# Moving a 32-row tile's products ahead of the last product of the first row pair

## The chip, the cores and the metric

The kernel runs on one core of a Trainium2 chip. A core has five engines that each take their instructions in order: TensorE (PE: matrix products, with weight loads listed as PEld), VectorE (DVE), ScalarE (ACT), GpSimd (POOL) and SyncE (SP). SP, POOL and ACT also issue DMA transfers; a transfer is "landed" when the engines that wait for it may go on. The metric is the device time of one execution in microseconds (us).

## The reference

One inference step of a small trunk, everything in float32. There are 2048 rows of a new stream (the prompt) and 32 rows of a running one (the sample), 1024 columns each. For each set of rows:

```
hn   = rmsnorm(h) * g_mix
proj = hn @ w_in                         # 1024 -> 3072, split in six parts of 512
yA   = B * (causal conv of C*h_in) * silu(zA)
yB   = (trailing means of v, minus v, mixed per group, scaled) * silu(zB)
h    = h + concat[yA, yB] @ w_out        # 1024 -> 1024: the output stage
gate = sigmoid(rmsnorm(h) * g_ple @ w_ple_gate)
h    = h + (p @ w_ple) * gate            # the gate stage
out  = rmsnorm(h) * g_final
```

The change concerns the line of the output stage: x + y @ w_out, above all for the 32 sample rows.

## The kernel before

**Stages.** The first stage (to about 531 us) makes y and stores it, channels first, in a buffer in device memory, `y_d`. The second makes products of p with w_ple for seven row tiles (names `e`, to 551 us). The output stage runs from 551 to 716 us. Then come the remaining `e` products and the gate stage.

**Precision.** Each product is made with operands split in a rounded half and the rest (`split`, L80: a cast on ACT, then a subtraction on DVE), and three of the four combinations are summed.

**Seven products for eight.** The output stage works on pairs of 128-row tiles, `for i in range(0, NT - 1, 2)` (L1468): pair 0, 2, ... 14. A pair of row tiles and two halves of the columns form a 2 x 2 block product, made in Strassen's way with seven products of 12 matmuls of 128x512 each (`seven`, L273). The frames are A["11"], "12", "22", S1 to S4; the weights are W["11"], "21", "22", T1 to T4. Three PSUM banks per pair, X, Y and Z, collect them; six banks exist (`ps_m`, L53). X is accumulated, carried out to SBUF (`carry`), accumulated on, summed into the rows of x (`out`), and so on: the last product of a pair, A["22"] x W["T4"], goes into X after `out(X, c3, (1, 1))` has read it. `step(n)` calls what the caller wants at that place of the pair.

**The first pair** is special: its weights are made while it runs, by ACT casts (L203), DVE differences (L195) and DVE subtractions (L210). Which weights come when is in the table LATER (L1455): T3 after the first product, 21 after the second, 22 later, T4 last.

**The 32-row tile.** `plain` (L342) makes its products without Strassen's scheme, from the weights 11, T1, 22 and 21, 32 matmuls in all (`packed`, L331: rounded half and rest side by side in one frame of 64 columns, then the rounded half with the weights' rest). `short` (L1351) splits its y, and `h_ops` with `two=True` (L1313) adds six DVE sums of 32x512. Before the change this ran after the pair i == 4:

```
            if last:
                n = tiles[NT - 1][1]
                A = short("yl", load_y(NT - 1, n), n)
```

**Buffers.** x rows are loaded into the pool `xh` (4 buffers), y into `ya` (5 buffers), split frames into `cmb`, the split short frame into `ss` (3 buffers), and `qa` (2 buffers) holds the first two `pps` operands of the `e` products and later rows of the gate weight (`gs`). At the start of the output stage two `xh` buffers hold rows of w_out (`wo_t`), two hold the first pair's x.

**Order.** A scheduler at build time decides in which order the instructions of an engine stand, from the program's order, the dependences and an estimate of times; at run time each engine keeps that order and waits where it must. `tc.issue_after` holds a load back behind a given instruction, `tc.keep_in_program_order` pins one.

**Lines to follow:** y loads L389, x loads L396, stores of h `done_h` L1340 to L1343, last rows of w_out `wo_b` L1410, load of g_final L1492, sums of `h_ops` L1315, the first pair's carries L1320, squares for the norm L94.

Of the kernel before, what the change touches and what calls it, by code (L numbers as in the profile page):

```python
# [9 lines left out]
F32 = mybir.dt.float32  # L10
# [5 lines left out]
P = 128  # L16
D = 1024
KC = D // P
SEQ = 2048
DEC = 32  # L20
# [8 lines left out]
NT = SEQ // P + 1  # L29
NH = D // 2  # L30
KH = KC // 2
# [5 lines left out]
def trunk(ctx, tc, x_p, x_s, c_conv, c_pool, p_p, p_s, g_mix, w_in, conv_w, conv_b, pool_w,  # L37
          pool_scale, w_out, g_ple, w_gate, w_ple, g_fin, y_p, y_s, sc_p, sp_p, sc_s, sp_s):
    nc = tc.nc
    x_p, x_s, p_p, p_s = x_p[0], x_s[0], p_p[0, 0], p_s[0, 0]  # L40
# [4 lines left out]
    y_d = tc.dram_tile([KC, P, T], F32, name="y_d")  # L45
# [34 lines left out]
    def split(hi, lo, src, eng=nc.vector, later=False):  # L80
        ins = nc.scalar.copy(hi, src)  # L81
        if later:
            tc.keep_in_program_order(ins)
        eng.tensor_tensor(lo, src, hi.bitcast(F32), op=ALU.subtract)  # L84
        return ins
# [15 lines left out]
    tiles = [(i * P, P) for i in range(SEQ // P)] + [(SEQ, DEC)]  # L101
# [128 lines left out]
    def frame_parts(cmb, tmp, name, a11, a12, a21, a22, *between):  # L230
# [3 lines left out]

        A = {}

        def put(q, src):
            A[q] = cmb.tile([P, KH, 2, P], F32R, tag="c", name=f"{name}_{q}")
            return split(A[q][:, :, 0], A[q][:, :, 1], src)

# [29 lines left out]

        return A, more

    def seven(name, A, W, carry, out, between={}, late=False, in_parts=False, first_tile=False, end=None):  # L273

        step = lambda c: between[c]() if c in between else None
        frames_late, weights_late = (FINE, FINE[::2] + FINE[1:2]) if in_parts else (None, None)
        X, Y, Z = (bank(f"{c}_{name}") for c in "xyz")

        def lower(*parts):
            for ks in parts:
                product(Z, A["S1"], W["T1"], P, ks.start == 0, ks)
            return carry(Z, (1, 1)) if ks.stop == KH else None

        parts = range(KH // 2), range(KH // 2, KH)
        product(X, A["11"], W["11"], P, True, order=frames_late)
        c1 = carry(X, (0, 0))
        step(1)

        def upper():
            product(Y, A["12"], W["21"], P, True, order=weights_late)
            out(Y, c1, (0, 0))

        if not late:  # L300
            upper()
        if late:
            lower(parts[0])
        step(2)
        product(X, A["S2"], W["T2"], P, False)
        c2 = carry(X, (0, 1))
        step(3)
        c3 = lower(parts[1]) if late else lower(range(KH))
        step(4)

        def right():
            product(Z, A["S4"], W["22"], P, False, order=weights_late)
            out(Z, c2, (0, 1))

        if first_tile:
            right()
        product(X, A["S3"], W["T3"], P, False)
        out(X, c3, (1, 1))
        step(5)
        if late:  # L320
            upper()
        if not first_tile:
            right()
        step(6)
        if end is not None:
            end(X)
            return
        product(X, A["22"], W["T4"], P, False)
        out(X, None, (1, 0))
# [12 lines left out]
    def plain(name, A, W, n, carry, out):  # L342

        X, Y, Z = (bank(f"{c}_{name}") for c in "xyz")
        packed(X, A[0], W["11"], n, True)
        c2 = carry(X, (0, 1))
        packed(Z, A[0], W["T1"], n, True)
        packed(Z, A[1], W["22"], n, False)
        out(Z, c2, (0, 1))
        packed(X, A[1], W["21"], n, False)  # L350
        out(X, None, (0, 0))
# [10 lines left out]
    def halves(t):  # L362

        return [t[:, c * KH * NH:(c + 1) * KH * NH].rearrange("p (k n) -> p k n", k=KH) for c in range(t.shape[1] // (KH * NH))]

    def seventh(name):
        return w7.tile([P, 2 * KH * NH], F32R, tag="h", name=name)
# [17 lines left out]
    def load_y(i, m, halves=2):  # L385
        a = early_y if i == 2 and halves == 2 else []
        for half in range(len(a), halves):
            t = ring4(ya, f"y_{i}_{half}").rearrange("p (k t) -> p k t", k=KH)
            nc.sync.dma_start(t[:, :, :m], y_d[half * KH:half * KH + KH, :, i * P:i * P + m].rearrange("k p t -> p k t"))  # L389
            a.append(t)  # L390
        return a

    def load_rows(pool, name, i, pr, sa=None, queue=nc.sync):
        r, n = tiles[i]
        t = ring4(pool, f"{name}_{i}")
        queue.dma_start(t[:n], pr[r:r + n] if sa is None else rows_of(pr, sa, r, n))  # L396
        return t
# [902 lines left out]
    with ExitStack() as s2:  # L1300
        pool = lambda name, bufs: s2.enter_context(tc.tile_pool(name=name, bufs=bufs, reuse_waits="tile"))
        qa, xh, ya, cmb = (pool(*a) for a in (("qa", 2), ("xh", 4), ("ya", 5), ("cmb", 8)))
# [10 lines left out]
        def h_ops(x, n, name, bare=False, two=False):  # L1313

            add = lambda o, a, b: nc.vector.tensor_tensor(o, a, b, op=ALU.add)  # L1315

            def carry(ps, at):
                t = st.tile([P, NH], F32, tag="t", name=f"c_{name}_{at[0]}{at[1]}")
                if bare and at != (1, 0):
                    nc.scalar.copy(t[:n], ps[:n])  # L1320
                    return t
                summed.append(add(t[:n], ps[:n], half_of(x, at, n)))
                if two:
                    add(t[:n], ps[n:2 * n], t[:n])
                return t

            def out(ps, c, at):
                t = half_of(x, at, n)
                if bare and at != (1, 0):
                    add(t, t, c[:n])  # L1330
                    c = None
                summed.append(add(t, ps[:n], t if c is None else c[:n]))
                if at == (0, 0):
                    first_sums.append(summed[-1])
                if two:
                    add(t, ps[n:2 * n], t)

            return carry, out

        def done_h(i, x):  # L1340
            r, n = tiles[i]
            sumsq(x, n, f"h{i}", rs_h[:, i:i + 1])
            (nc.gpsimd if 12 <= i < NT - 1 else nc.sync).dma_start(h_d[r:r + n], x[:n])  # L1343
# [7 lines left out]
        def short(name, parts, n):  # L1351

            A = []
            both = ss.tile([P, 2, KH, 2 * DEC], F32R, tag="s", name=f"{name}_a")
            for half, t in enumerate(parts):
                c = both[:, half]
                split(c[:, :, :n], c[:, :, n:2 * n], t[:, :, :n])
                A.append(c)
            return A
# [29 lines left out]
        S, W = {}, {}  # L1389
# [16 lines left out]
        bots, loaded = [], []  # L1406
# [10 lines left out]
        more = prep_h(0, lower_rows, lambda: lower_row(0))  # L1417
        weight_parts(W, tops, None, "11", "T1")
        W["21"] = halves(seventh("wo_21"))

        def early_ring(what, i):
            return space[:, i * D:i * D + D]

        _, run = embed(range(EARLY), wp, early_ring, nc.gpsimd, got=dict(enumerate(early_pps)))
        for c in range(EARLY):
            if c == EARLY - 2:
# [3 lines left out]
        st, ss = (s2.enter_context(tc.tile_pool(name=name, bufs=bufs, side="right", reuse_waits="tile"))  # L1430
                  for name, bufs in (("st", 4), ("ss", 3)))
        hold = []

        def later(*names):
            def run():
                for q in names:
                    if isinstance(q, int):
                        more(q)
                    else:
                        hold.append(weight_parts(W, tops, bots, q))  # L1440
            return run
# [10 lines left out]
            hold.append(weight_parts(W, tops, bots, "22", pin=True))  # L1452
            more(1)

        LATER = {1: third, 2: left, 3: right, 4: later("T4", 2)}  # L1455
        gate_rows = iter(range(KC))
        waiting = []


# [8 lines left out]
        for i in range(0, NT - 1, 2):  # L1468
            with tc.issue_after(loaded[0]):
                x = [load_rows(xh, "x", i + b, x_p) for b in range(2)] if i else first_x  # L1470
            seven(f"o{i}", S.pop(i), W, *h_ops(x, P, f"o{i}", i == 0), {0: LATER, **{p: {st: next_gate for q, st in GATE_STEPS if q == p} for p, _ in GATE_STEPS}}.get(i, {}), True)
            for b in range(2):
                done_h(i + b, x[b])
            last = i == 4
            if last:
                n = tiles[NT - 1][1]
                A = short("yl", load_y(NT - 1, n), n)
            if i + 2 < NT - 1:

                with tc.issue_after(loaded[0]), tc.issue_after(hold[-1].ins):  # L1480
                    more = prep_h(i + 2)
                for part in range(3):
                    more(part)
            if last:
                x = load_rows(xh, "x", NT - 1, x_p, x_s)
                plain("ol", A, W, n, *h_ops([x], n, "ol", two=True))
                done_h(NT - 1, x)
            if i == 0:
                next_gate()
            if i == 2:  # L1490
                with tc.issue_after(summed[-1].ins):
                    nc.sync.dma_start(g_bc, g_fin.partition_broadcast(P))  # L1492


        W = {}
# [298 lines left out]
        for i in range(0, NT - 3, 2):  # L1794
            A = S.pop(i)
# [38 lines left out]
```

## Time and profile before

| | |
|---|---|
| median of 3 runs | 932.08 us (931.37 to 932.5) |
| the profiled execution's own time | 929.11 us |
| its span, first to last instruction | 927.3 us |
| mean granted TensorE clock | 0.994 |
| output stage, first to last product | 550.9 to 716.2 us |
| the 32-row tile's products in it | 613.7 to 621.0 us |
| DMA over the span | 199.56 MB, mean 215 GB/s |

A row of the timeline gives start in us, busy time in us, engine, line, operation, output<-inputs by the program's names (numbers left out, so `x_o` is the bank X of any pair), tile shape and count of merged instructions; in brackets the idle time of the engine before it and what ended it. Rows of one engine that follow each other without idle time are merged as long as they are alike, so ends overlap a little with the next start. SPq, POOLq and ACTq are DMA issues. In a list of waits: who waited <- for whom: total us, times, longest. In a table by windows: the window, its length, busy time (and count) of the engines, the granted TensorE clock, the mean busy share of the 16 DMA engines, and GB/s.

### The profile page before, as it was taken

What the parts mean: (1) busy time and instruction counts of PE and PEld (TensorE: products, weight loads), DVE (VectorE), ACT (ScalarE), POOL (GpSimd) and SP (SyncE); (2) the same over time, 40 slices, a digit from 0 to 9 for tenths busy, and PEclk for the clock granted to TensorE, in tenths of its full rate; (3) what the DMA queues carried; (4) which work ended last, traced back from release to release, by engine and by line L of the source; (5) the groups of instructions that cost most, each with busy time, mean ns of one, the idle gap of its engine ahead of it and who ended that gap; (6) DMA issues with size and microseconds to landing.
All of it is one profiled execution on the core that took longest, in us unless ns stands there. A gap on an engine that the chain in (4) does not pass through costs nothing. (4 is left out here: it accounts for less than half of the span.)

```text
span 927.3 us, 12203 instructions
## 1 busy us (share of the span) xinstructions
PE 902.0 (97%) x4186; PEld 723.5 (78%) x4186; DVE 697.1 (75%) x1148; ACT 458.5 (49%) x828; POOL 158.9 (17%) x309
## 2 busy tenths in 40 slices
PE   8999999999999999999999998999999999999995
PEld 6788888878888788766688886878888778778885
DVE  6895789797993687746668679765655988888884
ACT  7752555465453354523344376434434965555553
POOL 2200121122121122100010021111111311121212
PEclk9999999999999999999999999999999999999998
DMA  8164396747599675777743695867768876476652
GB/s 277 47 206 169 104 270 188 227 153 235 174 339 428 165 226 177 246 219 236 235 145 131 225 320 166 264 224 238 223 220 276 306 249 193 165 227 206 218 186 105
DMA packets 113243, 199.56 MB, mean 215 GB/s; under 512 B 13206, under 2 KB 69950, under 8 KB 112157
## 3 DMA queue, kind: packets, MB, share of 16 engines
q1 hardware_dynamic: 88733, 117.19, 40.4%
q0 software_dynamic: 22000, 77.21, 24.6%
q10 hardware_dynamic: 2448, 4.39, 1.3%
q8 instruction: 33, 0.54, 0.2%
q14 instruction: 29, 0.24, 0.1%
HBM read 133.06 MB, written 65.67 MB: 214 GB/s over the span
## 5 line engine op out<-in xcount | busy, mean ns | idle before, releaser
L185 PE MATMUL x_o<-wo,y 128*128 128x512 f32 x192 | 47.1, 400 | 3.4 <-DVE x L1315 3.4
L185 PE MATMUL z_g<-wg,g_S 128*128 128x512 f32 x192 | 47.4, 393 | 0.7 <-ACT c_g L1558 0.7
L185 PE MATMUL z_o<-wo,y_S 128*128 128x512 f32 x192 | 47.4, 389 | 0.0
L185 PEld LDWEIGHTS x_o<-wo,y 128*128 128x128 f32 x192 | 37.1, 194 | 11.8 <-issue 3.8
L185 PE MATMUL x_o<-wo_T,y_S 128*128 128x512 f32 x192 | 46.2, 390 | 0.0
L185 PEld LDWEIGHTS z_g<-wg,g_S 128*128 128x128 f32 x192 | 35.5, 188 | 8.5 <-ACT c_g L1558 1.3
L646 PE MATMUL z_ch<-B,w_ch_S 128*128 128x512 f32 x168 | 40.8, 392 | 1.2 <-ACT U L966 1.2
L185 PEld LDWEIGHTS z_o<-wo,y_S 128*128 128x128 f32 x192 | 36.0, 188 | 7.5
L185 PEld LDWEIGHTS x_o<-wo_T,y_S 128*128 128x128 f32 x192 | 35.9, 188 | 7.6 <-DVE c_o L1315 0.2
L646 PE MATMUL x_ch<-B,w_ch_S 128*128 128x512 f32 x168 | 41.8, 392 | 0.0
L646 PE MATMUL x_zab<-B,w_zab_S 128*128 128x512 f32 x168 | 40.9, 392 | 0.2 <-DVE w_zab_S L84 0.2
L646 PE MATMUL z_zab<-B,w_zab_S 128*128 128x512 f32 x168 | 41.1, 392 | 0.0
L646 PE MATMUL x_zbv<-B,w_zbv_S 128*128 128x512 f32 x168 | 40.8, 391 | 0.0
L646 PE MATMUL z_zbv<-B,w_zbv_S 128*128 128x512 f32 x168 | 40.7, 391 | 0.0
L646 PEld LDWEIGHTS z_ch<-B,w_ch_S 128*128 128x128 f32 x168 | 31.3, 188 | 8.9 <-ACT U L966 1.6
L646 PEld LDWEIGHTS x_zab<-B,w_zab_S 128*128 128x128 f32 x168 | 31.3, 188 | 7.9 <-issue 0.8
L646 PEld LDWEIGHTS x_zbv<-B,w_zbv_S 128*128 128x128 f32 x168 | 31.3, 188 | 7.7 <-issue 0.8
L646 PEld LDWEIGHTS z_zab<-B,w_zab_S 128*128 128x128 f32 x168 | 31.2, 188 | 7.5 <-issue 0.8
L646 PEld LDWEIGHTS x_ch<-B,w_ch_S 128*128 128x128 f32 x168 | 31.3, 188 | 7.3 <-issue 0.8
L646 PEld LDWEIGHTS z_zbv<-B,w_zbv_S 128*128 128x128 f32 x168 | 31.3, 188 | 7.2 <-issue 0.8
L1577 DVE SCALAR_TENSOR_TENSOR h<-h,rstd_f,g_bc 128x1024 f32<-128x1024 f32 (+1 forms) x15 | 19.3, 1284 | 14.6 <-POOL rstd_f L77 13.0
L94 ACT ACTIVATE junk<-x 128x1024 bf16<-128x1024 f32 (+1 forms) x17 | 18.0, 1056 | 22.6 <-DVE x L1315 21.1
(561 smaller groups left out, 2297.9 us busy)
## 6 DMA issues: line engine op xcount, KB each, us to landing
wn<-in_w_in_dram SPq DMA_DIRECT2D x24, 512.0 KB, 3.8
p_dT<-T POOLq DMA_DIRECT2D x16, 512.0 KB, 5.2
y<-y_d SPq DMA_DIRECT2D x16, 512.0 KB, 5.9
h<-h_d POOLq DMA_DIRECT2D x16, 512.0 KB, 5.1
e<-e_d SPq DMA_DIRECT2D x15, 512.0 KB, 4.7
x<-in_x_prompt_dram SPq DMA_DIRECT2D x14, 512.0 KB, 4.0
out_dram<-h POOLq DMA_DIRECT2D x14, 512.0 KB, 3.4
B<-p_d POOLq DMA_DIRECT2D x3, 2048.0 KB, 15.7
```

What stands on the lines that cost most here:

```text
L94: ins = nc.scalar.activation(junk[:n], x[:n], AF.Square, accum_out=ssq[:n])
L185: nc.tensor.matmul(ps[:n], lhs[:, k, a, :n], w[b][:, k], start=start and k + q == 0, stop=k == KH - 1 and q == 2, skip_group_check=True)
L646: nc.tensor.matmul(ps, lhs[:, k, x], b[:, k, y], start=start and k + q == 0, stop=stop and k == KH - 1 and q == 2, skip_group_check=True)
L1577: nc.vector.scalar_tensor_tensor(h[:n], h[:n], rf[:n], g_bc[:n], op0=ALU.mult, op1=ALU.mult)
```

## The change

The 32-row tile leaves its place after pair 4. Its y is loaded in one transfer of 128 KB into a `qa` buffer (`short_y`, allowed after the last w_out row is issued), its x into an `xh` buffer ahead of the loop, and its products become step 6 of the first pair: in program order they stand after S4 x 22 and ahead of the last product, 22 x T4. Its rows of h are stored right behind the first pair's.

```diff
@@ -1417,6 +1417,9 @@
         more = prep_h(0, lower_rows, lambda: lower_row(0))
         weight_parts(W, tops, None, "11", "T1")
         W["21"] = halves(seventh("wo_21"))
+        short_y = qa.tile([P, KC, DEC], F32, tag="q", name="short_y")
+        with tc.issue_after(loaded[0]):
+            nc.sync.dma_start(short_y, y_d[:, :, SEQ:].rearrange("k p t -> p k t"))
 
         def early_ring(what, i):
             return space[:, i * D:i * D + D]
@@ -1430,6 +1433,7 @@
         st, ss = (s2.enter_context(tc.tile_pool(name=name, bufs=bufs, side="right", reuse_waits="tile"))
                   for name, bufs in (("st", 4), ("ss", 3)))
         hold = []
+        short_a = short("yl", (short_y[:, :KH], short_y[:, KH:]), DEC)
 
@@ -1452,8 +1456,14 @@
             hold.append(weight_parts(W, tops, bots, "22", pin=True))
             more(1)
 
-        LATER = {1: third, 2: left, 3: right, 4: later("T4", 2)}
+        last_n = tiles[NT - 1][1]
+
+        def short_tile():
+            plain("ol", short_a, W, last_n, *h_ops([short_x], last_n, "ol", two=True))
+
+        LATER = {1: third, 2: left, 3: right, 4: later("T4", 2), 6: short_tile}
         gate_rows = iter(range(KC))
+        short_x = load_rows(xh, "x", NT - 1, x_p, x_s)
         waiting = []
 
@@ -1471,20 +1481,14 @@
             for b in range(2):
                 done_h(i + b, x[b])
-            last = i == 4
-            if last:
-                n = tiles[NT - 1][1]
-                A = short("yl", load_y(NT - 1, n), n)
+            if i == 0:
+                done_h(NT - 1, short_x)
             if i + 2 < NT - 1:
 
                 with tc.issue_after(loaded[0]), tc.issue_after(hold[-1].ins):
                     more = prep_h(i + 2)
                 for part in range(3):
                     more(part)
-            if last:
-                x = load_rows(xh, "x", NT - 1, x_p, x_s)
-                plain("ol", A, W, n, *h_ops([x], n, "ol", two=True))
-                done_h(NT - 1, x)
             if i == 0:
                 next_gate()
```

## The prediction

> **What bounds the kernel now.** I read the page first, then the waits of TensorE in the output stage (530 to 720 us), then its timeline there, then what VectorE, ScalarE and the DMA queues did around the one wait that showed up.
>
> ```profile
> span 927.3 us, 12203 instructions
> PE 902.0 (97%) x4186; PEld 723.5 (78%) x4186; DVE 697.1 (75%) x1148; ACT 458.5 (49%) x828; POOL 158.9 (17%) x309
> ...
> PE x_o L185 <- DVE x L1315: 3.4, 1, 3.4
> ```
>
> TensorE (PE) is busy 97% of the span, so a change pays only where it closes one of PE's few holes. The last row is the whole list of PE's waits between 530 and 720 us: one, of 3.4 us, for a VectorE (DVE) sum of the first pair. The timeline shows where it is and what follows; the second number of a row is its busy time, and the windows give length, PE busy, granted clock, DMA share and GB/s.
>
> ```profile
> 567.50 0.61 PE L185 MATMUL x_o<-wo,y 128*128 128x512 f32 x2
> 571.53 6.88 PE L185 MATMUL x_o<-wo,y 128*128 128x512 f32 x22 [3.42 <-DVE x L1315]
> 578.24 1.53 PE L185 MATMUL z_o<-wo,y_S 128*128 128x512 f32 x6
> ...
> 591.90 5.60 PE L185 MATMUL x_o<-wo,y 128*128 128x512 f32 x24
> 597.34 1.52 PE L185 MATMUL z_o<-wo,y_S 128*128 128x512 f32 x6
> ...
> 613.66 1.08 PE L337 MATMUL x_ol<-wo,yl_a 128*64 128x512 f32 x4
> 621.02 2.90 PE L185 MATMUL x_o<-wo,y 128*128 128x512 f32 x12
> ...
> 571.50:575.00 3.50, 3.47 (x10) 0.60 0.96 256
> 575.00:579.00 4.00, 4.00 (x18) 0.92 0.62 180
> ```
>
> Undisturbed, 24 products go from 591.90 to 597.34: 5.44 us, 0.227 us each. At 567.50 two products of pair 2 are issued; the next, the first pair's last (T4), could start at 567.95 and starts at 571.53: a hole of 3.58 us. The 22 products behind it take 571.53 to 578.24, 6.71 us, where 22 x 0.227 = 4.99 would do: 1.72 us more, and the granted clock of these windows (0.60, then 0.92) says why. The hole costs 3.58 + 1.72 = 5.30 us. The short tile's 32 products stand at 613.66 to 621.02, 7.36 us (0.23 each), at full pace.
>
> The wait is for DVE, which is the bound of this stretch (columns: length, PE, PEld, DVE, ACT, POOL busy, clock, DMA):
>
> ```profile
> 551.00:571.50 20.50, 17.11 (x75) 13.54 (x74) 20.37 (x35) 13.05 (x25) 0.95 (x2) 1.00 0.54 199
> 571.50:590.00 18.50, 18.47 (x74) 15.00 (x75) 16.77 (x29) 10.93 (x20) 3.15 (x6) 0.91 0.78 233
> ...
> 570.11 0.68 DVE L1315 TENSOR_TENSOR x<-y_o,x 128x512 f32<-128x512 f32 x1
> 570.71 0.68 DVE L1315 TENSOR_TENSOR x<-x_o,x 128x512 f32<-128x512 f32 x1
> ```
>
> DVE works 20.37 of 20.50 us, making weight halves and frame halves, and only then comes to the sum at 570.71 that empties the bank into which T4 accumulates. Its rows follow each other at 0.60 us (570.11, 570.71).
>
> **The change part by part.** It adds no arithmetic. In the built order, the short tile's first 24 products stand between the first pair's S4 x 22 product and T4, then come 6 of T4, the other 8 short ones, 6 of T4, and pair 2, which no longer has two products ahead of T4. The first short product needs 11, T1 and 22, all used just before, and its own split.
>
> *The hole.* S4 x 22 ends at 567.50. 24 x 0.23 = 5.52 us of short products cover the time to 573.0, and T4's release comes at about 571.5 to 572, so about one us is left in hand. Removed: 5.30 us, the slow restart with the hole. At its old place the tile's 7.36 us vanish; they are paid here instead, part of them inside the hole, which the 5.30 already counts.
>
> *The split of y, moved ahead.* DVE gets two small subtractions and ScalarE (ACT) two small casts before the first pair's second half of weights.
>
> ```profile
> 550.66 1.07 ACT L167 COPY eouts<-e 128x512 f32<-128x512 f32 x2
> 553.82 0.59 ACT L1320 COPY c_o<-x_o 128x512 f32<-128x512 f32 x1 [2.09 <-PE x_o L185]
> 558.99 0.58 ACT L1320 COPY c_o<-x_o 128x512 f32<-128x512 f32 x1
> 559.74 2.93 PE L185 MATMUL x_o<-wo_T,y_S 128*128 128x512 f32 x12
> ...
> 586.11 0.50 ACT L81 CAST yl_a<-y 128x128 fp32r<-128x128 f32 x2 [1.51 <-DVE y_S L84]
> 586.60 0.28 DVE L84 TENSOR_TENSOR yl_a<-y,yl_a 128x128 fp32r<-128x128 f32 x1
> ```
>
> ACT's 0.50 us fall into its 2.09 us of idle before 553.82, ahead of the carry it stands before: free, and one for one on everything if y is late. DVE's 2 x 0.28 = 0.56 us go into a full queue. The delay reaches PE by a detour: ACT's fourth wo_T cast waits for DVE, the four casts of 21 and the carry at 558.99 stand behind it, and the product at 559.74 waits for the carry. Bounds 0 (some of it is taken out of the small waits) and 0.56; I take 0.3, since the carry before also had a little slack. Later products of the pair are no later than this.
>
> *The load of y.* One load of 128 KB on SP's queue takes the place of two of 64 KB.
>
> ```profile
> 536.00:551.00 15.00, 15.00 (x68) 12.43 (x67) 12.41 (x20) 11.62 (x22) 3.40 (x7) 1.00 0.92 310
> ...
> 533.23 1.30 SPq L1410 DMA_DIRECT2D wo_b<-in_w_out_dram  x3
> 542.09 0.55 POOL L1410 DMA_DIRECT2D wo_b<-in_w_out_dram  x1 [5.88 <-DMA y_d<-c_s]
> 542.27 0.33 SPq L1492 DMA_DIRECT2D g_bc<-in_g_final_dram  x1
> 549.41 0.69 DVE L195 TENSOR_TENSOR wo_t<-wo_b,wo_t 128x512 f32<-128x512 f32 x1 [0.70 <-DMA wo_b<-in_w_out_dram]
> ...
> wo_b<-in_w_out_dram SPq DMA_DIRECT2D x3, 512.0 KB, 8.8
> y<-y_d SPq DMA_DIRECT2D x2, 64.0 KB, 5.1
> ```
>
> It is issued right behind the three wo_b loads, about 534.6. Its landing lies between 534.6 + 5.1 = 539.7 and, if it starts only when those are done, 534.6 + 8.8 + 5.1 = 548.5, or 553.6 if twice the bytes take twice as long. ACT is free for it at 551.73. What it may delay is the fourth wo_b, for which DVE already waits 0.70 at 549.41: between 0 and 5.1 us. I take 0: SP's queue carried g_bc beside that load before, and y goes in ahead of it. Queued behind it on SP is only g_bc, issued at 542.27 for a reason of its own.
>
> *x and the stores.* The 32 rows of x take one of the two early buffers, so pair 2's second x must wait until the first pair's first row of tiles is stored.
>
> ```profile
> 573.21 0.33 SPq L1343 DMA_DIRECT2D h_d<-x  x1
> 579.82 0.34 SPq L396 DMA_DIRECT2D x<-in_x_prompt_dram  x1
> 584.20 0.68 DVE L1315 TENSOR_TENSOR c_o<-z_o,x 128x512 f32<-128x512 f32 x1
> ...
> h_d<-x SPq DMA_DIRECT2D x1, 512.0 KB, 6.5
> x<-in_x_prompt_dram SPq DMA_DIRECT2D x1, 512.0 KB, 3.3
> ```
>
> Store at about 573.6, landed 6.5 us later (580.1), load issued behind it on SP, landed 3.3 later: 583.4, or 585 if the larger y load now ahead of the store costs 1.5. The sum that reads it (584.20 before) is due at about 586 in the new DVE order, and PE needs the bank that it empties at about 591. Cover: 1 to 7 us; cost 0. Behind that load on SP stand the stores of the short rows and of the pair's second tile, pair 6's second y and pair 4's x; the first of these that PE needs is pair 4's x, for a carry at about 577.9 + 96 x 0.227 = 599.7, some 8 us after it can land (store 582, landed 588, load 592).
>
> *The six sums of the short tile.* 6 x 0.60 = 3.6 us move from an idle stretch into 571 to 578.
>
> ```profile
> 615.71 0.68 DVE L1315 TENSOR_TENSOR c_ol<-x_ol,x 32x512 f32<-32x512 f32 x1 [0.42 <-PE x_ol L340]
> ```
>
> Counting the new DVE order from 569.9 at this pitch: T4's last sum at 578.5, pair 2's S1 half ready at 580.4, its first carry at 582.2. PE, from 567.8: T4 done 577.9, first product of pair 2 done 580.6, S1's half needed at 581.1, the carry at 582.9. Both have 0.7 us to spare: cost 0 to 3.6 - 0.7 = 2.9 us, taken as 0.
>
> *Sum.* 5.30 - 0.3 = 5.0 us. Counted forward instead: pair 6 begins at 577.9 + 168 x 0.227 = 616.0 instead of 621.02, again 5.0.
>
> *Does it last?* DMA is near full before the gate stage, so I looked at what starts its loads.
>
> ```profile
> SPq L1504 <- PE x_o L185: 3.7, 1, 3.7
> 720.00:725.00 5.00, 3.42 (x20) 2.76 (x19) 4.93 (x9) 3.98 (x8) 2.79 (x6) 1.00 0.98 353
> 724.30 16.60 PE L109 MATMUL e<-wq,pps 128*128 128x512 f32 x72 [1.57 <-DMA pps<-pp_d]
> ```
>
> The loads of wq wait for PE's products, so the crowd moves with PE; I carry all 5.0 us to the end. The profiled execution took 929.11 us (1.8 around its span), so 924.1 by its own time. The runs shown have a median of 932.08, 2.97 above it; the same 5.0 off gives **927.1 us**.
>
> The Trainium skill (page "TensorE: Matmul & The Clock Gate", section "Part 1: The HAM clock gate") says that the array falls to half rate after an idle window of about 3.4 us, and that the window runs free of the kernel. The trace agrees: 0.60 after the hole of 3.4, 1.00 after the wait of 1.57. By that rule a hole of just this length might in some executions not trip it.
>
> **The rivals.**
>
> *B, DVE takes over.* The moved sums make pair 2's halves late, or the fourth wo_b lands later. For it: DVE is full, and 0.7 us of slack is little. Against: from 571.5 to 590 DVE had 1.7 us of idle and ACT 7.6. Price half of 2.9: gain 3.5, 928.6; at its worst 2.1, 930.0.
>
> *C, no slow restart in the timed runs.* If the clock did not fall there, only 3.58 - 0.3 = 3.3 is won: 928.8. Against: the three times of before lie within 1.13 us, less than the 1.72 that would part them. The rule named above is what makes this possible.
>
> *D, slower: y is late.* The two casts stand ahead of ACT's first carry, and ACT runs in order; each us by which y lands after about 552 holds the carry, the casts of the weights and so PE. Up to 557 it eats the gain, beyond it the kernel is slower; landed at 559, 25 us after issue: 934. For it: DMA is busy 0.92 of 536 to 551 and the load has 1024 runs of 128 bytes. Against: the 64 KB loads with the same runs landed in 5.1.
>
> *E, the hole is not filled.* If a bank or the split holds the first short product until DVE is through, the hole only changes its place: 932.1. Against: six banks, of which the first pair holds three.
>
> **How the numbers follow.** Forecast 0.62, B 0.17, C 0.05, E 0.07, D 0.09. The forecast's own range is 926.4 to 927.9 (DVE's cost 0 to 0.56 and the scatter of the runs). With B and C nearly whole, the range is 926.2 to 929.9. What a measurement of this kernel can tell from no change is about 0.2%, 1.9 us: faster is the forecast, B and C, 0.84; same is E, 0.07; slower is D, 0.09.
>
> **What would show it.** Right: no PE wait over 0.5 us between 550 and 620, short products from about 567.8, granted clock 1.00 in 570 to 580, pair 6 beginning near 616 and the later stages about 5 us earlier. Wrong: ACT waiting on the load of short_y (D), PE waiting on a DVE sum or half after 577 (B), a hole ahead of the first short product (E), or a larger wait on pps near 719 that gives the gain back.

## The result, and the profile after

| | before | after |
|---|---|---|
| median | 932.5 us (931.37 to 933.27) | 928.56 us (925.46 to 929.51) |
| the profiled execution's own time | 929.11 us | 928.58 us |
| its span | 927.3 us | 926.7 us |

The ratio is 0.996, with a 95% interval of 0.9943 to 0.9978: faster, by 2 to 5 us. The forecast, a gain of 5.0 of 932.08 us, is a ratio of 0.9946 and lies inside that interval; the median itself, 928.56, lies outside the forecast's own range (926.4 to 927.9) and where rival B was priced (928.6), so this result alone does not part the two. The two spans differ by 0.6 us only, so the first question is where the rest of the forecast 5.0 is in this one execution. The page of after begins with:

```profile
span 926.7 us, 12196 instructions
...
PE 902.3 (97%) x4186; PEld 723.5 (78%) x4186; DVE 697.2 (75%) x1148; ACT 459.6 (50%) x828; POOL 160.2 (17%) x309
```

PE has the same 4186 matmuls and nearly the same busy time (902.3 against 902.0); time at a lower clock counts as busy. The place of the hole, in the timeline of after:

```profile
567.06 2.88 PE L185 MATMUL z_o<-wo,y_S 128*128 128x512 f32 x12
569.78 1.08 PE L337 MATMUL x_ol<-wo,yl_a 128*64 128x512 f32 x4
...
574.38 1.09 PE L340 MATMUL z_ol<-wo,yl_a 128*32 128x512 f32 x4
575.31 1.54 PE L185 MATMUL x_o<-wo,y 128*128 128x512 f32 x6
576.69 1.08 PE L337 MATMUL x_ol<-wo,yl_a 128*64 128x512 f32 x4
```

The short tile's 24 products stand where the hole was, 569.78 to 575.31, then six of T4, then the other eight, as forecast. The windows of the prediction (length, PE, PEld, DVE, ACT, POOL busy, granted clock, DMA share, GB/s) now read:

```profile
551.00:571.50 20.50, 19.65 (x87) 15.40 (x86) 20.02 (x35) 14.54 (x28) 1.06 (x2) 1.00 0.48 172
571.50:590.00 18.50, 18.50 (x83) 13.62 (x82) 18.27 (x30) 7.19 (x13) 5.04 (x8) 1.00 0.82 268
```

PE is busy 38.15 of these 39.00 us (35.58 before), and the clock is 1.00 in the second row (0.91 before). All of PE's waits from 530 us to the end, in after (total, times, longest):

```profile
PE pth L1536 <- ACT ho L1534: 1.9, 2, 1.4
PE e L109 <- DMA pps<-pp_d: 1.9, 1, 1.9
PE x_g L185 <- DVE c_g L1570: 0.9, 1, 0.9
PE y_o L185 <- DVE wo L210: 0.9, 1, 0.9
PE z_g L185 <- ACT c_g L1562: 0.7, 1, 0.7
```

The 3.4 us of DVE's sum (L1315) are gone. A wait of 0.9 on weights (`wo`) is new and lies ahead of the short tile; the others belong to the `e` products and the gate stage. That new wait in the timelines of PE, DVE and the list of transfers (us from issue to landing) of after:

```profile
560.43 0.39 PE L185 MATMUL y_o<-wo,y 128*128 128x512 f32 x1
561.67 0.50 PE L185 MATMUL y_o<-wo,y 128*128 128x512 f32 x1 [0.85 <-DVE wo L210]
...
551.48 0.69 DVE L195 TENSOR_TENSOR wo_t<-wo_b,wo_t 128x512 f32<-128x512 f32 x1 [1.40 <-DMA wo_b<-in_w_out_dram]
554.50 0.49 DVE L84 TENSOR_TENSOR yl_a<-short_y,yl_a 128x128 fp32r<-128x128 f32 x2
...
wo_b<-in_w_out_dram POOLq DMA_DIRECT2D x1, 512.0 KB, 7.9
```

DVE waited 1.40 us for the fourth wo_b (0.70 before); the split of y adds 0.49. Last, PE's timeline of after where the output stage ends (the `e` products begin at 713.19), and its windows behind the wait on pps (length, PE busy, clock, DMA share, GB/s):

```profile
713.19 5.61 PE L109 MATMUL e<-wq,pps 128*128 128x512 f32 x24
718.64 1.03 PE L1536 MATMUL pth<-ident,ho 128*128 128x128 f32 x8
721.57 18.20 PE L109 MATMUL e<-wq,pps 128*128 128x512 f32 x72 [1.89 <-DMA pps<-pp_d]
739.61 2.01 PE L137 MATMUL e<-wq,pps 128*64 128x512 f32 x8
...
722.00:724.00 2.00, 2.00 (x8) 0.65 1.03 413
724.00:726.00 2.00, 2.00 (x7) 0.50 1.04 424
```

The same 72 products took 16.60 us before, at a clock of 1.00 from the start. So the slow restart that went with the hole came back 150 us later, behind a wait of 1.89 us where 1.57 had not brought it.

This gives the account of the two profiled executions. F is the start of the first product of the output stage, G that of the first 24 `e` products behind it, H that of the eight `e` products (739.61 above), L that of the last six matmuls (`e_l`).

| | before | after | difference |
|---|---|---|---|
| F, where the change has not yet come | 550.90 | 552.27 | +1.37 |
| G - F, the output stage | 165.34 | 160.92 | -4.42 |
| H - G, the wait on pps and the products around it | 24.49 | 26.42 | +1.93 |
| L - H, the gate stage | 176.13 | 176.64 | +0.51 |
| sum | 916.86 | 916.25 | -0.61 |

The output stage won 4.42 of the forecast 5.0. The rest of the difference between the spans is a later start, a wait on a transfer and a slow restart. The later start is not the change's: the first `wo_b` loads, which stand ahead of its first instruction, are issued at 534.64 already (533.23 before). Whether the latter belong to the change or to these two executions is what the experiments had to tell.

### The profile page after: what moved, and what is told of

Same layout as the page of the kernel before. It is cut to its first block, busy times and chain, and to the rows that moved or that the text cites. A ratio compares the mean times of both kernels' runs of the same rounds, so it can differ in the third digit from the quotient of the medians.

```text
span 926.7 us, 12196 instructions
## 1 busy us (share of the span) xinstructions
PE 902.3 (97%) x4186; PEld 723.5 (78%) x4186; DVE 697.2 (75%) x1148; ACT 459.6 (50%) x828; POOL 160.2 (17%) x309
## 3 DMA queue, kind: packets, MB, share of 16 engines
q10 hardware_dynamic: 2448, 4.39, 1.3%
## 4 chain that ended last, share of the span: by engine, by line
PE 56%; DMA 11%; issue 5%; DVE 3%; ACT 2%; POOL 1%; POOLq 0%; ACTq 0%; DVEq 0%; SPq 0%
PE x_g L185 7%; PE x_o L185 7%; PE x_zab L646 5%; PE x_zbv L646 4%; PE x_ch L646 4%; PE z_g L185 4%; DMA raw_zab_0b<-in_w_in_dram 4%; PE z_o L185 3%; PE e L109 3%; PE z_zab L646 2%; PE z_ch L646 2%; PE z_zbv L646 2%; PE y_o L185 2%; PE y_g L185 2%; DMA hn<-h_d 2%
## 5 line engine op out<-in xcount | busy, mean ns | idle before, releaser
L185 PE MATMUL x_o<-wo,y 128*128 128x512 f32 x192 | 45.2, 389 | 0.0
L81 ACT CAST y_S<-y_fS 128x512 fp32r<-128x512 f32 x28 | 17.1, 621 | 28.9 <-PE x_o L185 12.5
```

Of the source, the lines that this page charges most:

```text
L185: nc.tensor.matmul(ps[:n], lhs[:, k, a, :n], w[b][:, k], start=start and k + q == 0, stop=k == KH - 1 and q == 2, skip_group_check=True)
```

## The experiments

Twelve kernels ran, in three groups of four (1 to 4; 5, 8, 9 and 11; 6, 7, 10 and 12). Each group ran beside runs of the kernel before, with medians of 931.29, 931.1 and 930.98 us, and its ratios are to those. The first table has the kernels before and after and the first four; "landing" is the time from issue to landing of the fourth wo_b, and what stands behind the ratio is from one profile each.

| kernel | median us | ratio to before, 95% interval | G - F | landing | wait on pps | the 72 products |
|---|---|---|---|---|---|---|
| before | 932.5 | | 165.34 | 7.3 | 1.57 | 16.60 |
| after | 928.56 | 0.996 (0.9943 to 0.9978) | 160.92 | 7.9 | 1.89 | 18.20 |
| 1: after again | 926.56 | 0.9942 (0.9922 to 0.9962) | 160.64 | 6.9 | 2.33 | 16.58 |
| 2: hole filled with transposes | 929.45 | 0.998 (0.9965 to 0.9994) | 163.83 | 6.3 | 1.71 | 16.60 |
| 3: loads only | 931.0 | 1.0007 (0.9991 to 1.0022) | 165.67 | 6.9 | 2.35 | 18.20 |
| 4: y ahead of w_out | 925.12 | 0.9934 (0.9914 to 0.9954) | 160.38 | 4.4 | 1.10 | 16.60 |

**1. The changed kernel again**, beside the variants.

> The changed kernel once more, as the yardstick of this call. Theory 1 (the hole in the first pair and the slow restart behind it are removed, 4.4 us in the output stage; a slow restart can come back behind PE's 1.9 us wait for pps near 720 us, 1.6 us, in some executions): 927 to 929, with its profile either showing clock 0.5 to 0.65 near 722 to 726 or, if not, the 72 products there in 16.4 us and a span some 1.6 us shorter. Rival (the lost 1 us is the early y load alone): the clock near 720 is 1.00 and the time the same 928.5.

0.9942. In its profile the wait for the fourth wo_b is small, and the wait on pps is longer than in after, yet nothing is slow behind it (DVE, PE, and a window of PE):

```profile
549.92 0.69 DVE L195 TENSOR_TENSOR wo_t<-wo_b,wo_t 128x512 f32<-128x512 f32 x1 [0.30 <-DMA wo_b<-in_w_out_dram]
...
721.26 16.58 PE L109 MATMUL e<-wq,pps 128*128 128x512 f32 x72 [2.33 <-DMA pps<-pp_d]
...
722.00:724.00 2.00, 2.00 (x10) 1.00 1.05 420
```

So the restart in after is not a fixed price of the change: the same instructions have it in one execution and not in another. It is not the whole of the difference either: this span is 921.7 us, 5.0 less than after's, and 3.11 of that lie in the gate stage (L - H is 173.53 against 176.64).

**2. Only the restart taken away.** The kernel before, with 30 transposes of the identity in the hole, whose result nothing reads. The release of T4 isn't touched.

```diff
-        LATER = {1: third, 2: left, 3: right, 4: later("T4", 2)}
+        LATER = {1: third, 2: left, 3: right, 4: later("T4", 2), 6: lambda: fill(30, tbank("warm_hole"))}
```

> The kernel before, with 30 transposes of the identity in the hole ahead of the first pair's last product and nothing else. Theory 1: the hole keeps its 3.4 us but the clock stays at 1.00, the 22 products behind it take 5.0 us instead of 6.7, and the gate stage begins 1.7 us earlier; the end moves by 1.7 or, where the clock falls behind the pps wait, by about 0: 930.5 to 932.5. Rival (the slow products are held by DVE, not by the clock): they stay at 6.7 us and the time at 932.5.

Its timeline, PE and the DVE sum that releases T4:

```profile
568.39 3.44 PE L452 MATMUL warm_hole<-ident 128*128 128x128 f32 x30
571.58 6.09 PE L185 MATMUL x_o<-wo,y 128*128 128x512 f32 x24
577.51 1.68 PE L185 MATMUL z_o<-wo,y_S 128*128 128x512 f32 x6
...
571.59 0.68 DVE L1315 TENSOR_TENSOR x<-x_o,x 128x512 f32<-128x512 f32 x1
```

In before the 22 products start 0.82 us after the start of that sum (570.71 to 571.53); by the same step they start here at 572.41, 20.62 us after F (20.63 before), and take 5.10 us to 577.51 instead of 6.71. (The first two of the 24 at 571.58 are pair 2's, ahead of T4.) So the restart costs 6.71 - 5.10 = 1.61 us in this place (forecast: 1.72), G - F falls by 1.51, and the time by 0.2% (0.06 to 0.35%). It is a cost of its own, in timed runs too.

**3. Only the loads and the split moved.** The early load of y, its split and the early x, with the products left behind pair 4:

```diff
-        LATER = {1: third, 2: left, 3: right, 4: later("T4", 2), 6: short_tile}
+        LATER = {1: third, 2: left, 3: right, 4: later("T4", 2)}
...
-            if i == 0:
-                done_h(NT - 1, short_x)
...
+            if i == 4:
+                short_tile()
+                done_h(NT - 1, short_x)
```

> The early load and split of y and the early load of x, but the 32 products at their old place behind pair 4. Theory 1: the hole is there again, moved by the 0.5 to 0.9 us that the split and the late wo_b cost, slow restart too: 932.5 to 934, pair 6 begins some 70.5 us after the stage's first product instead of 70.1. Rival (the gain comes from the tile's old place being cheaper without its loads): 928 to 930.

The hole is back, with its restart (PE):

```profile
567.82 0.61 PE L185 MATMUL x_o<-wo,y 128*128 128x512 f32 x2
571.86 6.86 PE L185 MATMUL x_o<-wo,y 128*128 128x512 f32 x22 [3.42 <-DVE x L1315]
578.56 1.52 PE L185 MATMUL z_o<-wo,y_S 128*128 128x512 f32 x6
```

G - F is 0.33 longer than before, the time 1.0007 of it. So the early loads by themselves change the time by no more than 2 us either way (interval 0.9991 to 1.0022) and win nothing, and the gain comes with where the products stand. Of that 0.33, 0.30 are there at the third group of products of the stage, behind a wait of 0.81 us of DVE for the fourth wo_b and the split; in experiment 1, where DVE waited 0.30, they are not.

**4. y loaded earlier, and g_bc later.** The changed kernel with y in the free half of `g_bc`. The load of g_final into `g_bc` then has to wait for the split of y, so two transfers move.

```diff
-        short_y = qa.tile([P, KC, DEC], F32, tag="q", name="short_y")
-        with tc.issue_after(loaded[0]):
+        short_y = g_bc[:, NH:NH + KC * DEC].rearrange("p (k t) -> p k t", k=KC)
+        with tc.issue_after(last_raw):
```

> The changed kernel, with y loaded some 15 us earlier into a free part of g_bc, ahead of the w_out rows. Theory 1 with contention (the y load of 1024 runs holds up the fourth wo_b by 0.6 us): DVE's wait for wo_b falls from 1.4 to about 0.8, the product with T3 starts 9.2 us after the stage's first instead of 9.7, 0.5 us gained: 928.0 against 928.5. Rival (wo_b's lateness is chance of the execution): no change in either.

The list of transfers, and the issue of g_bc's load in the timeline:

```profile
wo_b<-in_w_out_dram POOLq DMA_DIRECT2D x1, 512.0 KB, 4.4
...
542.72 0.55 POOL L1410 DMA_DIRECT2D wo_b<-in_w_out_dram  x1 [6.67 <-DMA y_d<-c_s]
552.12 0.33 SPq L1496 DMA_DIRECT2D g_bc<-in_g_final_dram  x1
```

With g_bc's 512 KB issued 9.4 us behind the fourth wo_b instead of 0.1, wo_b lands in 4.4 us and DVE doesn't wait for it. G - F is 160.38, 4.96 less than before. Whether y or g_bc is the cause, this doesn't tell.

**5 and 6. g_bc later, alone: missed.** Two tries to hold back only g_bc's load, first by an `issue_after` on the part T3, then by its place in the program.

```diff
-                with tc.issue_after(summed[-1].ins):
+                with tc.issue_after(summed[-1].ins), tc.issue_after(hold[0].ins):
...
-            if i == 2:
+            if i == 4:
```

> The changed kernel with one edit: the 512 KB load of g_bc waits for the end of the part T3 of the weight rows, so it runs after the fourth wo_b has landed; the early load of y stays. In the profiled changed kernel the fourth wo_b landed 7.9 us after its issue and DVE waited 1.40 us for it; with y moved ahead and g_bc's load displaced at the same time it landed after 4.4 us and nothing waited. Theory G (g_bc's load is what slows wo_b): wo_b lands after 4.4 to 5 us, DVE's wait for it is gone, the third group of products starts 8.8 us after the first product of the output stage, and the time is that of the variant with y ahead, about 925 us against 926.6 to 928.6 of the changed kernel. Theory Y (y's load is what slows it): it still lands after about 7 us or more with a wait of 0.3 to 1.4 us, and the time stays at 926.6 to 928.6. This edit changes no arithmetic.

> The changed kernel with the load of g_bc taken up one row pair later in the program (the try before it left that load's issue at 543.56 us, where it had been, and so told nothing of it); y's early load stays as it is. In the profiles the fourth wo_b, 512 KB, lands 6.3 to 7.9 us after its issue in all kernels that issue g_bc's 512 KB beside it, with the early y (6.4 to 7.9) and without it (6.3 and 7.3), and after 4.3 and 4.4 us in the two that issue g_bc some 9 us later. Theory G (g_bc's load alone slows it): it lands after 4.2 to 5 us, DVE has no wait for it, the third group of products starts 8.8 us after the first product of the output stage. Theory Y (y's early load slows it too): it lands after more than 6 us and DVE waits 0.2 us or more. By theory G the time is at most 0.9 us below the changed kernel's in the same call, and 0 to 0.4 in the middle, since two of the changed kernel's three profiles lost nothing there. This edit changes no arithmetic.

Neither moved the transfer; the first row is of the first try, the second of the second:

```profile
543.56 0.33 SPq L1496 DMA_DIRECT2D g_bc<-in_g_final_dram  x1
```

```profile
543.58 0.33 SPq L1496 DMA_DIRECT2D g_bc<-in_g_final_dram  x1
```

After issues it at 543.68, right behind wo_b's 543.57. On every engine the instructions stand as in the changed kernel, so these are two more samples of it, and neither theory was put to the test.

**7. The changed kernel a third time.**

> The changed kernel a third time, beside the variants of this call. If its gain over the kernel before is about 5 us with about 1 us of scatter between executions (a slow restart of 1.6 us behind the wait on pps and a wait of 2 us on hn that come and go), the ratio is 0.994 to 0.996, 926 to 928 us. Forecast on record: a gain of 5.0 us, ratio 0.9946. If the first result (3.9 us) is the whole of it, 0.996 or more.

0.9944; the forecast is 0.9946. All five samples of the changed kernel's order, with T the start of the third group of products in the output stage (in after's timeline, the 12 x_o<-wo_T,y_S behind 561.67):

| | median us | ratio, 95% interval | T - F | G - F | landing | wait on pps | 72 products | L - H |
|---|---|---|---|---|---|---|---|---|
| before | | | 8.84 | 165.34 | 7.3 | 1.57 | 16.60 | 176.13 |
| after | 928.56 | 0.996 (0.9943 to 0.9978) | 9.74 | 160.92 | 7.9 | 1.89 | 18.20 | 176.64 |
| 1 | 926.56 | 0.9942 (0.9922 to 0.9962) | 8.84 | 160.64 | 6.9 | 2.33 | 16.58 | 173.53 |
| 5 | 925.97 | 0.9948 (0.993 to 0.9966) | 8.85 | 160.60 | 6.4 | 2.92 | 18.18 | 173.62 |
| 6 | 925.44 | 0.9938 (0.9923 to 0.9952) | 8.84 | 160.12 | 6.5 | 2.09 | 18.20 | 173.55 |
| 7 | 925.9 | 0.9944 (0.993 to 0.9958) | 8.84 | 160.06 | 6.4 | 3.09 | 17.98 | 173.76 |

The mean of the five ratios is 0.9946, and 0.9946 lies in each interval. G - F fell by 4.42 to 5.28 us, 4.87 on average. The 0.9 us at T are in one profile of these five. (In 5 the profile puts the wait of 2.92 down to a weight half that DVE makes, `wq`, not to pps; the 72 products stand behind it all the same.)

**8. Transposes in the wait on pps.** The changed kernel with 20 transposes ahead of the 72 products.

```diff
         for c in range(len(rest_e)):
+            if c == 2:
+                fill(20, bank("warm_e"))
```

> The changed kernel with 20 transposes of the identity, whose result nothing reads, put into PE's wait for the third pps of the second embedding; the wait itself stays 1.6 to 2.4 us long. Theory 1 (behind the wait some executions lose 1.6 us to a slow restart, others none): the granted clock stays 1.00 behind the wait, the products take 16.4 to 16.6 us, and the median falls by 0 to 1.6 us, with the slowest runs falling most: 926 to 927.5 us. Rival (the 18.04 us were contention and not the clock): the products take 18 us in some executions still, and the time stays at 926.6 to 928.6 us. The transposes are added work.

926.06 us, ratio 0.9945 (0.9929 to 0.9961). PE:

```profile
717.61 2.34 PE L452 MATMUL warm_e<-ident 128*128 128x128 f32 x20
719.79 0.38 PE L1536 MATMUL pth<-ident,ho 128*128 128x128 f32 x2
721.75 8.43 PE L109 MATMUL e<-wq,pps 128*128 128x512 f32 x36 [1.57 <-DMA pps<-pp_d]
```

36 products in 8.43 us are full pace. But one profile without a slow restart proves little where experiment 1 had none either, and the median is that of the changed kernel (925.97 and 926.56). It doesn't show a gain.

**9 and 10. The third pps ahead of the rows of the gate weight (`wg_b`)**, to take the wait away; run twice.

```diff
-        with tc.issue_after(second_pps.ins):
+        got[2] = st.tile([P, 2, 2, P], F32R, tag="t", name=f"pps_{EARLY + 2}")
+        third_pps = load_pps(got[2], EARLY + 2, nc.sync, True)
+        with tc.issue_after(third_pps.ins):
```

> The changed kernel with the third pps of the second embedding loaded ahead of the wg_b rows on SP's queue. The profiles show a PE wait of 1.6 to 2.4 us on that load in all six executions, and behind it in two of the six the 72 products take 18.04 to 18.2 us of granted clock 0.65 and 0.50 at first instead of 16.4 to 16.6. Theory 1 (the wait costs its length on the chain, and in some executions a slow restart of 1.6 us besides): the wait is gone, the 72 products take 16.4 to 16.6 us, and the time is 1.5 to 3.5 us below the changed kernel, 923 to 925 us. Rival (the wg_b rows, now later, hold PE in the gate stage instead): the wait on pps goes, but the gate stage has a new wait of 1 to 3 us on the wg parts, and the time stays within 1 us of 926.6 to 928.6. This edit changes no arithmetic.

> The variant with the third pps ahead of the wg_b rows again, beside the changed kernel. In its first profile the wait on pps did not go: 2.04 us, now on the fourth pps. Theory D (the transfers run at their full rate in this stretch, 412 to 424 GB/s at a share of 1.0, so their order moves the wait and doesn't remove it): a wait of 1.5 to 2.5 us on pps again, and the time within 1 us of the changed kernel's. Rival (the wait is shorter in sum, or the gate stage is better off): 1.5 to 2.5 us below the changed kernel's, as the first call's medians were (923.94 against 925.97 of the kernel of the same instructions).

923.94 us (0.9925, 0.9909 to 0.994) and 923.71 us (0.9918, 0.99 to 0.9937). (The expectation puts the wait at 1.6 to 2.4 us in six executions; in experiment 4 it was 1.10.) The theory that the wait goes was wrong: it moved to the fourth pps, 2.04 us in the first run and 2.49 in the second, whose timeline and windows are:

```profile
712.31 8.33 PE L109 MATMUL e<-wq,pps 128*128 128x512 f32 x36
723.79 5.72 PE L109 MATMUL e<-wq,pps 128*128 128x512 f32 x24 [2.49 <-DMA pps<-pp_d]
...
722.00:724.00 2.00, 0.21 (x1) 1.00 1.05 416
724.00:726.00 2.00, 2.00 (x10) 1.00 1.03 412
```

The DMA share is 1.03 to 1.05 there, so the DMA engines have no free time to give; the new order moved the wait and didn't shorten it. Yet the times are some 2 us below the changed kernel's of the same groups (925.97 and 925.9).

**11 and 12. Both together:** experiment 4 with 9, and 6 with 9. As 6 changed nothing, the second is a third sample of 9.

> The two edits together on the changed kernel: y loaded ahead into the free half of g_bc (which also puts g_bc's load behind the split of y), and the third pps loaded ahead of the wg_b rows. If the wait for the fourth wo_b and the wait on pps are independent, the gains add: about 1.4 us below the changed kernel for the first (925.1 against 926.6 in the same call) and 1.5 to 3.5 us for the second, 921.5 to 923.5 us. If something else ends the later stages (a wait on wg parts, or a hn load) the second gain is lost and the time is that of the first alone, 925 us. This edit changes no arithmetic.

> g_bc's load one row pair later and the third pps ahead of the wg_b rows, together on the changed kernel. By theory G and theory D: no wait for the fourth wo_b, a wait of 1.5 to 2.5 us on pps, time 0 to 1 us below the changed kernel's of this call. By their rivals 2 to 3 us below it, 923 to 924 us.

924.06 us (0.993, 0.991 to 0.9951) and 925.39 us (0.9934, 0.9919 to 0.995). The gains don't add. In the first the fourth wo_b again lands early, in 4.3 us; both have the wait on pps and a slow restart. PE and its window, of the second:

```profile
725.45 7.09 PE L109 MATMUL e<-wq,pps 128*128 128x512 f32 x24 [4.39 <-DMA pps<-pp_d]
...
726.00:728.00 2.00, 2.00 (x6) 0.50 1.02 410
```

The three samples of 9 have a mean of 924.35 us, those of the changed kernel in the same two groups (5, 6, 7) 925.77: 1.4 us, with intervals that overlap. The wait is not shorter (2.04, 2.49 and 4.39 against 2.92, 2.09 and 3.09); the restart was there in one profile of three against three of three. What makes 9 faster, if it is, stays open.

## Why the prediction was right

**The hole, 5.30 us: right, in both terms.** After's waits have nothing on the sum of L1315, and the clock is 1.00 from 571.5 to 590. The split into 3.58 and 1.72 holds too: the transposes took away the second term alone and won 1.51 us of G - F, and rival C (no slow restart in the timed runs) falls with it, since those runs were 0.2% faster. The prediction's own reason against C does not carry: that the three times of before lay within 1.13 us was luck, as the 23 runs of the same kernel beside experiments 1 to 4 spread from 928.83 to 933.26. Where PE waits for nothing in the output stage (experiments 6 and 7) G - F is 5.22 and 5.28 less than before: the hole's whole price.

**The split of y ahead on DVE, 0.3 us: mis-sized in both directions.** Measured at T: 0.9 in the first profile, outside the stated 0 to 0.56, and 0.0 in the four others. Its route was wrong too. The prediction had PE wait for a carry on ACT; in after PE waits 0.85 for a weight that DVE makes (`y_o`, L210). And what made DVE late was less the split (0.49) than the fourth wo_b, for which it waited 0.70 us longer than before. Experiment 10, whose edit only moves loads near the end of the output stage, has the same delay in small (DVE, PE):

```profile
550.64 0.69 DVE L195 TENSOR_TENSOR wo_t<-wo_b,wo_t 128x512 f32<-128x512 f32 x1 [1.22 <-DMA wo_b<-in_w_out_dram]
...
560.82 0.50 PE L185 MATMUL y_o<-wo,y 128*128 128x512 f32 x1 [0.66 <-DVE wo L210]
```

With the early split, waits of DVE of 1.40 (after), 1.22 and 0.81 us (experiment 3) go with a T - F that is 0.90, 0.71 and 0.30 above 8.84, so 0.50 less each time, and waits up to 0.36 with none. So the split cost nothing where the fourth wo_b was on time, and showed where that was late as well.

**The load of y, 0 us: right.** With the early y the fourth wo_b lands after 6.3 to 7.9 us, without it after 7.3 (before) and 6.3 (experiment 2); experiment 3, which has all the early loads, is at 1.0007. Two profiles without the early y are few to tell small delays by. Rival D needed y after 557; DVE subtracts its halves from 554.50 on (the row above), so D is out.

**x, the stores, the six sums, 0 us: right.** PE has no wait between 561.67 and the `e` products. Pair 6 begins 12 matmuls behind this row of after's timeline,

```profile
615.27 5.60 PE L185 MATMUL x_o<-wo,y 128*128 128x512 f32 x24
```

at 615.27 + 12 x 0.227 = 617.99, 65.72 us after F, where 70.12 stood before: 4.40 less, and that is G - F's 4.42. Nothing is lost in between, so rival B (DVE takes over after 577) and rival E (the hole moves) are out. B's sign shows in small in two of the five: at 659 us PE waits 0.36 us (experiment 1) and 0.29 us (experiment 5) for a sum of L1315, against B's price of 1.45.

**"I carry all 5.0 us to the end": right in the timed mean, not in the profiled execution.** There the last sign that the prediction gave for being wrong came up: more wait on pps (0.32) and 1.6 us of slow restart behind it gave 1.93 back. The five samples have H - G of 26.42, 25.23, 27.42, 26.62 and 27.39 against 24.49 in the one profile of before, and L - H near 173.6 in four of them against 176.13. The kernels 2 and 3, which have the order of before in that stretch, have 24.63 and 26.87, and 173.87 and 173.92. So both stages jump by 2 us and more in either order, and one profile of before can't say whether the change shifts the odds. In the gate stage the jump goes with a load of rows of h (`hn`). Before and experiment 1, ACT and PE:

```profile
751.48 1.14 ACT L1530 COPY ho<-hn 128x512 f32<-128x512 f32 x2 [4.01 <-DMA hn<-h_d]
752.15 1.18 PE L1532 MATMUL pth<-ident,ho 128*128 128x128 f32 x8 [1.22 <-ACT ho L1530]
```

```profile
745.59 1.14 ACT L1534 COPY ho<-hn 128x512 f32<-128x512 f32 x2 [2.02 <-DMA hn<-h_d]
```

ACT waits 4.01, 5.04 and 3.51 us for it in before, after and experiment 4, whose L - H is 176.13 to 176.64, and at most 2.02 us in all other kernels, which have 172.69 to 173.92. By the medians little is lost: the forecast ratio is the mean of the five.

The first result's 3.9 us instead of 5.0 is therefore no missing mechanism that could be shown: its interval takes in 0.9946, and four more samples stand at 0.9938 to 0.9948. That the mean of the five meets the forecast to the last digit is luck, as each interval is some 3 us wide.

## What to carry to other kernels

A short hole of PE has a second price, the slow restart; work that is due anyway, moved into the hole, wins both, while filler wins only the second (4.9 against 1.5 us here). Look for such work whose operands are the ones just used and whose inputs can be early at no cost, and check the early loads by themselves. And compare two profiles by stages, each from its own start: here the stage ahead of the change differed by 1.37 us between two executions and the stages behind it by 2, as much as what was to be seen.

## What the hardware showed that was not expected

**The clock falls behind waits shorter than the hole, and not always.** Behind the wait on pps (eight transposes or six, about 1 us, then the idle time) the granted clock fell after waits of 1.89, 2.09, 2.35, 2.42, 2.92, 3.09 and 4.39 us, and stayed at 1.00 after 1.10, 1.57, 1.71, 2.04, 2.33 and 2.49. Up to 1.71 it never fell (three profiles), from 2.92 on always (three), and between the length doesn't decide. The Trainium skill (page "TensorE: Matmul & The Clock Gate", section "Part 1: The HAM clock gate") says that the window that the gate watches runs free of the kernel; that fits a band in which the same wait goes either way. The same section of the Trainium skill gives about 3.4 us for the idle window: here 1.89 us without any matmul, behind 1.03 us of small ones, were enough, and the measurement decides.

**A 512 KB load landed later in every kernel that issued another beside it.** The fourth wo_b landed 6.3 to 7.9 us after its issue in all twelve kernels that issue g_bc's load next to it, and after 4.4 and 4.3 us in the two that issue it 9 to 10 us later. These two also load y earlier, but y's load by itself left the landing where it was, so g_bc's load is the likely cause. That is argued and not shown: by itself it was not moved in any run.
